# A streaming encoder step on one core: the normalization of v's last pair moved behind the first weight operands

## The chip, the cores and the metric

The kernel runs on one core of one Trainium2 chip. The metric is device time in microseconds (us) for one execution; lower is better. Five engines take part: TensorE (PE in the profile; its weight loads are PEld), VectorE (DVE), ScalarE (ACT), GpSimd (POOL) and SyncE (SP, which here only issues DMAs). Each engine runs its own instructions strictly in the order in which they were built, and waits for the others on semaphores.

## The reference, cut to what matters

One layer over 4096 prompt rows (and 32 sample rows), width 1024, everything in float32:

```python
h = rmsnorm(x, norm_g)
u, v, z_a, xb, z_b = jnp.split(h @ w_in, 5, axis=-1)        # five projections of width 1024
v_n = layernorm(v, ln_v_g, ln_v_b)
a = u * chunk_mlp(v_n, w_spatial, b_spatial) * silu(z_a)    # 128x128 mixing per head and chunk
b = pool_mix(x_ext, pos0, w_pool, pool_scale) * silu(z_b)   # trailing means, a linear map per group
y = x + concat([a, b]) @ w_out
return rmsnorm(y, final_g)
```

For this change the middle line counts: every row of v has its mean subtracted and is divided by its standard deviation, and the result is needed by the gate branch `a` only.

## The kernel before, in words

**Arithmetic.** A float32 product is made of three passes of a faster number format: each operand is split into a high part (rounded by ACT, L109 `nc.scalar.copy`) and a low part (the remainder, taken by DVE, L82 `lo_part`). Products of 2x2 blocks are formed by a scheme with seven products instead of eight. So each set of 128 output columns has seven products, numbered q = 0 to 6; one product is 12 matmuls of 128x512 (`product`, L184). Its weights are the tiles `wop`, one for each q, and some of them are sums of raw weight blocks which DVE forms first (L105, tiles `sum` and `raw`).

**Stages.** First v is computed for all rows, two row tiles (a "pair") at a time, into the SBUF tiles `vt`. Then `norms` normalizes a pair: on DVE four `BN_STATS` (L298), two `BN_AGGR` (L299), a short chain for the reciprocal root (L87 to L92), and the factors `nb` (L308); on ACT two `ACTIVATE`s of 128x1024 (L310), one for each `vt`. `Pair.store` then sends the two `vt` to DRAM (`v_all`, L489) from POOL's queue. The last two pairs are `pa` and `pb`. After v, four token blocks of 1024 rows each run through 16 "sets" of weights: 8 gate sets and 8 pool sets.

**The seam.** The first group of sets is two pool sets, called A and B here, which need no v. Their fourteen steps are interleaved by `lagged`; the first five are A0, A1, B0, A2 and B1. `prepare(n)` emits the weight operands up to step n, `LEAD = 5` is how far ahead of the products it runs, and `norms(..., behind=True)` with `store` finishes v. `tc.issue_after` and `tc.keep_in_program_order` are directions to the scheduler that orders each engine's instructions. A scheduler, not the source alone, decides the final order. As built, TensorE goes through the products in the order A0, A1, B0, B1, A3, A2, B2, A4, A5, B3, (transposes of the spatial weights WT, L823), A6, B4, B5, (L837), B6, and then the first gate set. The names of their weights are:

- before: A0 `wop_3686`, A1 `wop_3689`, B0 `wop_3721`, B1 `wop_3760`, A3 `wop_3792`, A2 `wop_3757`, B2 `wop_3814`, B5 `wop_3924`, B6 `wop_3944`
- after: the same, but B1 is `wop_3731` and A2 is `wop_3728`

**Accumulators.** Six PSUM banks hold the sums (`Combine`). q = 0 opens a bank; ACT copies it out (L158, `t<-acc`); then q = 2 and q = 4 add to the same bank. So product A2 cannot start before ACT has copied A0's sum (`t_3808<-acc_3795`). Likewise q = 6 adds to the bank that q = 3 opened, after DVE has read it (L156). For B6 that read is `t_4080<-acc_3970`.

**Queues behind the seam.** The sets' raw weights and v rows come by SP's queue: L811 loads WT, L812 the bias, L793 a few columns, L870 rows of `v_all` (after the stores of v have landed), and L877 raw weights. The loads of `raw_3962` and `raw_3964`, the weights of the second gate set, stand behind the first L870 on that queue.

Of the kernel before, what the change touches and what calls it, by code (L numbers as in the profile page):

```python
# [15 lines left out]
P = 128  # L16
# [19 lines left out]
def stream_step(ctx: ExitStack, tc, x_prompt, x_sample, state_pool, norm_g, w_in, ln_v_g, ln_v_b,  # L36
# [9 lines left out]
    nc = tc.nc  # L46
# [31 lines left out]
    def small(tag, n, rows=P):  # L78
        return smallp.tile([P, 8], F32, tag=tag, name=tag)[:rows, :n]
# [4 lines left out]
    def rsqrt(a, n, rows=P):  # L84

        y, t = small("rs_y", n, rows), small("rs_t", n, rows)
        nc.vector.tensor_single_scalar(t.bitcast(I32), a.bitcast(I32), 1, ALU.logical_shift_right)  # L87
        nc.vector.tensor_scalar(y.bitcast(I32), t.bitcast(I32), -1.0, float(0x5F3759DF), ALU.mult, ALU.add)
        for _ in range(3):
            nc.vector.tensor_tensor(t, y, y, ALU.mult)  # L90
            nc.vector.scalar_tensor_tensor(t, t, -0.5, a, ALU.mult, ALU.mult)
            nc.vector.scalar_tensor_tensor(y, t, 1.5, y, ALU.add, ALU.mult)  # L92
        return y
# [5 lines left out]
    behind, newest = [], {}  # L99
# [103 lines left out]
    def pool(name, bufs, stack=ctx, **kw):  # L203
        return stack.enter_context(tc.tile_pool(name=name, bufs=bufs, reuse_waits="tile", **kw))
# [4 lines left out]
    with ExitStack() as ph:  # L209
# [73 lines left out]
        def norms(xs_, vs_, behind=False):  # L283

            nx, nv, n = len(xs_), len(vs_), len(xs_) + len(vs_)
            rows = (xs_ + vs_)[0][1]
            a = small("na", n, rows)
            if xs_:
                ss = small("ss", nx, rows)
                for i, (xt, _) in enumerate(xs_):  # L290
                    junk = h_p.tile([P, D], BF16, tag="junk", name="junk", bufs=1)
                    nc.scalar.activation(junk[:rows], xt[:rows], AF.Square, accum_out=ss[:, i:i + 1])
            if vs_:
                st = smallp.tile([P, 2, 2, 6], F32, tag="bn", name="bn")
                mv = smallp.tile([P, 2, 2], F32, tag="mv", name="mv")
                for i, (v, _) in enumerate(vs_):
                    for z in range(2):
                        nc.vector.bn_stats(st[:rows, i, z, :], v[:rows, z * 512:(z + 1) * 512])  # L298
                    nc.vector.bn_aggr(mv[:rows, i, :], st[:rows, i].rearrange("p z c -> p (z c)"))  # L299
                nc.vector.tensor_scalar_add(a[:, nx:], mv[:rows, :nv, 1], EPS)  # L300
            if xs_:
                nc.vector.tensor_scalar(a[:, :nx], ss, 1.0 / D, EPS, ALU.mult, ALU.add)
            r = rsqrt(a, n, rows)
            for i, (xt, _) in enumerate(xs_):
                nc.vector.scalar_tensor_tensor(xt[:rows], xt[:rows], r[:, i:i + 1], g_bc[:rows], ALU.mult, ALU.mult)
            if vs_:
                nb = small("nb", nv, rows)
                nc.vector.scalar_tensor_tensor(nb, mv[:rows, :nv, 0], -1.0, r[:, nx:], ALU.mult, ALU.mult)  # L308
                for i, (v, _) in enumerate(vs_):
                    act = nc.scalar.activation(v[:rows], v[:rows], AF.Identity, scale=r[:, nx + i:nx + i + 1],  # L310
                                               bias=nb[:, i:i + 1])
                    if behind:
                        tc.keep_in_program_order(act)
# [224 lines left out]
        pa, pb = pairs[-2:]  # L538
# [261 lines left out]
    with ExitStack() as ph:  # L800
# [333 lines left out]
        def prepare(upto):  # L1134

            nonlocal done
            while done < min(upto, len(steps)):
                while loads and loads[0][0] <= done + (AHEAD if done < first[id(groups[n_sets][0])] + 7 else 6):
                    loads.pop(0)[2].load()
                s, q = steps[done]  # L1140
                s.prep[q]()
                if done in beside:
                    w, q = beside[done]
                    w.prep[q]()
                done += 1

        tokens[0].ops = first_ops
        for s in groups[0]:
            loads.pop(0)[2].load(nc.gpsimd)
        for n, pair in ((2, pa), (3, pb)):  # L1150
            prepare(n)
            norms([], [(v, P) for v in pair.v], behind=True)
            pair.store(nc.gpsimd)
        with tc.issue_after(newest["lo"]):
            prepare(LEAD)
        v_stack.close()
        t_p = pool("t_p", 10, ph)
        cn_p = pool("cn_p", 1, ph)
# [156 lines left out]
```

## Time and profile before

| what | value |
|---|---|
| time, median of 3 runs | 2327.71 us (2327.01 to 2328.79) |
| profiled execution | 2331.34 us |
| its span on the core | 2329.6 us |
| PE busy | 2312.3 us, 99% |
| DVE busy | 1761.1 us, 76% |
| ACT busy | 893.6 us, 38% |
| granted TensorE clock, mean | 0.999 |

How to read the profile's lines: a timeline row has the start in us from the span's start, the length in us, the engine, the line of the kernel, the operation, the tiles (out<-in), shapes, and xN for a run of equal instructions; in square brackets stands the idle time of the engine before it and who ended that. SPq is a DMA issue on SP's queue. A row of the waits has the total in us, the number of times, and the longest. The row "PEclk" of a page and the column PEclk of a table by stretches are the granted clock of TensorE as a share of full speed.

### The profile page before, as it was taken

How to read it: one execution, taken by the hardware profiler on the slowest of the kernel's cores; microseconds unless marked ns; L12 is line 12 of the kernel's file. 1: busy time of each engine (PE TensorE's matmuls, PEld its weight loads, DVE VectorE, ACT ScalarE, POOL GpSimd, SP SyncE). 2: the span in 40 equal slices, each digit the busy share in tenths (PEclk: the TensorE clock that was granted, in tenths of full speed). 3: DMA queues.
4: the chain of work that ended last, by engine and by line, in shares of the span. 5: the costliest groups of instructions: out<-in, count | busy, mean ns of one | idle time of the engine just before them, and what ended most of it. 6: DMA issues, size and time to landing. Idle time of an engine off the chain costs nothing.

```text
span 2329.6 us, 30101 instructions
## 1 busy us (share of the span) xinstructions
PE 2312.3 (99%) x10722; PEld 1891.8 (81%) x10722; DVE 1761.1 (76%) x3171; ACT 893.6 (38%) x1560; POOL 229.4 (10%) x357
## 2 busy tenths in 40 slices
PE   8999999999999999999999999999999999999998
PEld 6888888878778888788878888888888777887887
DVE  6887777868787866787767967768876666588887
ACT  6554544334334333443434433434322222233343
POOL 1000000000131002221000211001100000000000
PEclk9999999999999999999999999999999999999999
DMA  9877877445548454566544393535485665856552
GB/s 309 303 271 276 294 244 248 136 161 172 170 153 334 149 179 140 197 225 230 190 159 143 118 331 107 194 118 167 180 340 169 214 205 197 334 163 204 178 168 90
DMA packets 320365, 474.95 MB, mean 204 GB/s; under 512 B 27324, under 2 KB 226492, under 8 KB 318424
## 3 DMA queue, kind: packets, MB, share of 16 engines
q1 hardware_dynamic: 269016, 383.96, 48.3%
q0 software_dynamic: 21936, 74.14, 8.7%
q10 hardware_dynamic: 29264, 14.94, 2.4%
q8 instruction: 84, 1.38, 0.2%
q14 instruction: 65, 0.53, 0.1%
HBM read 303.51 MB, written 169.47 MB: 203 GB/s over the span
## 4 chain that ended last, share of the span: by engine, by line
PE 97%; DMA 1%; DVE 1%; ACT 0%; issue 0%; SPq 0%; ACTq 0%; DVEq 0%
PE acc L184 65%; PE acc L665 9%; PE acc L667 9%; PE acc L666 9%; PE sp L918 2%; PE tr L428 1%; PE acc L192 1%; DMA vt<-in_w_in_dram 1%; PE acc L259 1%; PE more L192 1%; DMA op<-in_w_in_dram 0%; DMA wops<-wop 0%; DVE wop L82 0%; PE tr L380 0%; DVE slot L82 0%
## 5 line engine op out<-in xcount | busy, mean ns | idle before, releaser
L184 PE MATMUL acc<-slot,wop 128*128 128x512 f32 x5376 | 1240.7, 391 | 0.8 <-DVE wop L82 0.4
L184 PEld LDWEIGHTS acc<-slot,wop 128*128 128x128 f32 x5376 | 1003.4, 188 | 225.7 <-DVE t L156 9.6
L82 DVE TENSOR_TENSOR wop<-raw,wop 128x512 fp32r<-128x512 f32 x520 | 353.9, 685 | 47.2 <-ACT wop L109 39.2
L109 ACT CAST wop<-raw 128x512 fp32r<-128x512 f32 x360 | 221.1, 622 | 332.2 <-PE acc L184 253.0
L665 PE MATMUL acc<-slot,wop 128*128 128x512 f32 x892 | 348.4, 391 | 0.0
L667 PE MATMUL acc<-slot,wop 128*128 128x512 f32 x892 | 347.1, 389 | 0.0
L666 PE MATMUL acc<-slot,wop 128*128 128x512 f32 x892 | 347.0, 389 | 0.0
L184 PE MATMUL acc<-slot,op 128*128 128x512 f32 x1344 | 323.2, 395 | 1.3 <-ACT op L434 1.1
L184 PEld LDWEIGHTS acc<-slot,op 128*128 128x128 f32 x1344 | 247.8, 188 | 52.7 <-ACT op L434 1.6
L156 DVE TENSOR_TENSOR t<-acc,t 128x512 f32<-128x512 f32 x256 | 175.5, 685 | 139.6 <-ACT t L165 102.5
L677 DVE TENSOR_TENSOR y<-acc,y 128x512 f32<-128x512 f32 x243 | 164.4, 687 | 134.6 <-PE acc L667 133.6
L665 PEld LDWEIGHTS acc<-slot,wop 128*128 128x128 f32 x892 | 167.4, 188 | 44.7 <-ACT wop L628 10.1
L628 ACT CAST wop<-raw 128x512 fp32r<-128x512 f32 x160 | 99.4, 621 | 253.6 <-PE acc L667 231.5
L667 PEld LDWEIGHTS acc<-slot,wop 128*128 128x128 f32 x892 | 167.4, 188 | 34.9
L666 PEld LDWEIGHTS acc<-slot,wop 128*128 128x128 f32 x892 | 167.4, 188 | 34.5
L82 DVE TENSOR_TENSOR wop<-sum,wop 128x512 fp32r<-128x512 f32 x208 | 142.3, 686 | 66.0 <-ACT wop L109 64.9
L926 POOL DMA_DIRECT2D abT<-t x128 | 69.3, 542 | 798.5 <-DVE t L936 542.3
L109 ACT CAST wop<-sum 128x512 fp32r<-128x512 f32 x144 | 89.1, 622 | 148.9 <-PE acc L184 99.1
L947 DVE TENSOR_TENSOR t<-t 128x527 f32<-128x527 f32 (+3 forms) x160 | 111.1, 695 | 0.4
L165 ACT COPY t<-acc 128x512 f32<-128x512 f32 x64 | 37.5, 586 | 126.9 <-PE acc L184 126.9
L628 ACT CAST wop<-sum 128x512 fp32r<-128x512 f32 x64 | 39.8, 621 | 105.3 <-PE acc L667 70.6
L920 DVE SCALAR_TENSOR_TENSOR t<-sp,lvg,bias 128x512 f32<-128x512 f32 x64 | 47.7, 745 | 42.0 <-PE sp L918 41.9
(201 smaller groups left out, 1875.7 us busy)
## 6 DMA issues: line engine op xcount, KB each, us to landing
raw<-in_w_in_dram SPq DMA_DIRECT2D x134, 512.0 KB, 4.7
xops<-op SPq DMA_DIRECT2D x100, 512.0 KB, 6.5
slot<-xops SPq DMA_DIRECT2D x44, 1024.0 KB, 9.5
abT<-t POOLq DMA_DIRECT2D x128, 256.0 KB, 3.0
raw<-abT SPq DMA_DIRECT2D x64, 512.0 KB, 5.2
wops<-wop SPq DMA_DIRECT2D x56, 512.0 KB, 3.4
slot<-wops SPq DMA_DIRECT2D x14, 2048.0 KB, 9.6
raw<-comb SPq DMA_DIRECT2D x38, 512.0 KB, 4.4
```

The source lines that it names most:

```text
L82: return nc.vector.tensor_tensor(out, src, hi.bitcast(F32), ALU.subtract)
L109: pair = nc.scalar.copy(hi, src), lo_part(lo, src, hi)
L156: add = lambda o, x, y: nc.vector.tensor_tensor(o, x, y, ALU.add)
L184: mm(acc, stationary(s, k), moving(m, k), start=fresh and n == 0, stop=n == len(terms) - 1, skip_group_check=True)
L628: nc.scalar.copy(t[:, 0], src)
L665: mm(acc, x[:, 0, k, :], w[:, k, 0, c], start=fresh and k == 0, stop=False, skip_group_check=True)
L666: mm(acc, x[:, 0, k, :], w[:, k, 1, c], start=False, stop=False, skip_group_check=True)
L667: mm(acc, x[:, 1, k, :], w[:, k, 0, c], start=False, stop=k == 3, skip_group_check=True)
L677: nc.vector.tensor_tensor(y, self.acc[bank], y, ALU.add)
L920: nc.vector.scalar_tensor_tensor(t1[:, :HALF].rearrange("p (a c) -> p a c", c=P), sp, lg, bias[:, h:h + 1, :].broadcast_to([P, 4, P]), ALU ...
L926: nc.gpsimd.dma_start(abT[row, :, t0:t0 + HALF], t[:, :HALF])
L947: tt(nxt[:, lo:HALO + m], s[:, lo:HALO + m], s[:, lo - step:HALO + m - step], ALU.add)
```

## The change

The loop over the two pairs is written out, and for `pb` the order is turned: before, `norms` and `store` of `pb` came right after `prepare(3)` and ahead of `prepare(LEAD)`; now `prepare(LEAD)` comes first, `norms` of `pb` follows inside the same `issue_after` block, and the store follows that. Nothing is computed differently and no instruction is added or removed.

```diff
-        for n, pair in ((2, pa), (3, pb)):
-            prepare(n)
-            norms([], [(v, P) for v in pair.v], behind=True)
-            pair.store(nc.gpsimd)
+        prepare(2)
+        norms([], [(v, P) for v in pa.v], behind=True)
+        pa.store(nc.gpsimd)
+        prepare(3)
         with tc.issue_after(newest["lo"]):
             prepare(LEAD)
+            norms([], [(v, P) for v in pb.v], behind=True)
+        pb.store(nc.gpsimd)
```

What stands on DVE where `pb`'s chain ended, before. `vt_3355` and `vt_3356` are `pb`'s two tiles; `rs_t`, `rs_y` and `nb_3747` are its chain, `raw` and `sum` the raw blocks and block sums of sets A and B:

```order
L91 SCALAR_TENSOR_TENSOR rs_t_3735<-rs_t_3735,na_3724 128x2
L82 TENSOR_TENSOR wop_3721<-raw_3682,wop_3721 128x512
L92 SCALAR_TENSOR_TENSOR rs_y_3734<-rs_t_3735,rs_y_3734 128x2
L105 TENSOR_TENSOR sum_3753<-raw_3680,raw_3678 128x512
L90 TENSOR_TENSOR rs_t_3735<-rs_y_3734 128x2
L105 TENSOR_TENSOR sum_3754<-raw_3680,sum_3753 128x512
L91 SCALAR_TENSOR_TENSOR rs_t_3735<-rs_t_3735,na_3724 128x2
L105 TENSOR_TENSOR raw_3680<-raw_3680 128x512
L92 SCALAR_TENSOR_TENSOR rs_y_3734<-rs_t_3735,rs_y_3734 128x2
L105 TENSOR_TENSOR sum_3810<-raw_3684,raw_3682 128x512
L308 SCALAR_TENSOR_TENSOR nb_3747<-mv_3726,rs_y_3734 128x2
L82 TENSOR_TENSOR wop_3757<-sum_3754,wop_3757 128x512
```

Four large operations (128x512) stand between B0's low part `wop_3721` and `nb_3747`; by then the four `BN_STATS` are done. The low part of A2 comes behind `nb`.

What stands there now, from B0's low part on:

```order
L82 TENSOR_TENSOR wop_3721<-raw_3682,wop_3721 128x512
L105 TENSOR_TENSOR sum_3724<-raw_3680,raw_3678 128x512
L298 BN_STATS bn_3735<-vt_3355 128x6
L105 TENSOR_TENSOR sum_3725<-raw_3680,sum_3724 128x512
L298 BN_STATS bn_3735<-vt_3355 128x6
L298 BN_STATS bn_3735<-vt_3356 128x6
L82 TENSOR_TENSOR wop_3728<-sum_3725,wop_3728 128x512
L82 TENSOR_TENSOR wop_3731<-raw_3682,wop_3731 128x512
L299 BN_AGGR mv_3736<-bn_3735 128x2
L298 BN_STATS bn_3735<-vt_3356 128x6
L105 TENSOR_TENSOR raw_3680<-raw_3680 128x512
L299 BN_AGGR mv_3736<-bn_3735 128x2
```

All four `BN_STATS` now stand behind B0's low part, and the low parts of A2 and B1 ahead of the chain. The chain's steps follow, each between two large operations (`sum_3810`, `wop_3792`, `raw_3684`, `raw_3678`, `sum_3811`, `raw_3682`), and it ends in eight small steps in a row with `nb_3757` as the last, ahead of `t_3808<-acc_3817`.

ACT's order around `pb`'s two `ACTIVATE`s (before it is the same, with the names of before):

```order
L109 CAST wop_3792<-raw_3680 128x512
L310 ACTIVATE vt_3355<-vt_3355,nb_3757,rs_y_3744 128x1024
L310 ACTIVATE vt_3356<-vt_3356,nb_3757,rs_y_3744 128x1024
L158 COPY t_3808<-acc_3795 128x512
L109 CAST wop_3814<-sum_3811 128x512
```

The `ACTIVATE`s have kept their place on ACT: the copy of A0's sum still stands behind them, and B2's cast behind that.

Further on, DVE's order where the second gate set's first sum `sum_4240` stood before, behind L955:

```order
L105 TENSOR_TENSOR raw_3834<-raw_3834 128x512
L156 TENSOR_TENSOR t_3941<-acc_3894,t_3939 128x512
L82 TENSOR_TENSOR wop_4022<-raw_3832,wop_4022 128x512
L947 TENSOR_TENSOR t_4043<-t_3808 128x527
L105 TENSOR_TENSOR raw_3832<-raw_3832,sum_4053 128x512
L156 TENSOR_TENSOR t_3939<-acc_3947,t_3939 128x512
L947 TENSOR_TENSOR t_4045<-t_4043 128x525
L82 TENSOR_TENSOR wop_4056<-sum_4053,wop_4056 128x512
L955 SCALAR_TENSOR_TENSOR t_4045<-t_4045,t_3808 128x496
L105 TENSOR_TENSOR sum_4240<-raw_3964,raw_3962 128x512
L824 MEMSET WT_3787 64x4x64
```

And now:

```order
L82 TENSOR_TENSOR wop_3967<-raw_3832,wop_3967 128x512
L105 TENSOR_TENSOR sum_4240<-raw_3964,raw_3962 128x512
L156 TENSOR_TENSOR t_3941<-acc_3894,t_3939 128x512
L82 TENSOR_TENSOR wop_4022<-raw_3832,wop_4022 128x512
L947 TENSOR_TENSOR t_4043<-t_3808 128x527
L105 TENSOR_TENSOR raw_3832<-raw_3832,sum_4053 128x512
L156 TENSOR_TENSOR t_3939<-acc_3947,t_3939 128x512
L947 TENSOR_TENSOR t_4045<-t_4043 128x525
L82 TENSOR_TENSOR wop_4056<-sum_4053,wop_4056 128x512
L955 SCALAR_TENSOR_TENSOR t_4045<-t_4045,t_3808 128x496
L105 TENSOR_TENSOR sum_4241<-raw_3964,sum_4240 128x512
L824 MEMSET WT_3787 64x4x64
```

`sum_4240`, which waits for the loads of `raw_3964` and `raw_3962`, has moved up by eight large operations, ahead of `t_3941<-acc_3894`, and `sum_4241` has taken its old place. The order of TensorE, POOL and SP is unchanged; on ACT a few casts further on changed places with copies.

## The prediction

> **What bounds the kernel now.** I read the page first, then the waits of TensorE, then the timelines of PE, ACT, DVE and the queues around the seam between v and the first sets. The page, with its span, its PE row and the chain that ended last:
>
> ```profile
> span 2329.6 us, 30101 instructions
> PE 2312.3 (99%) x10722; PEld 1891.8 (81%) x10722; DVE 1761.1 (76%) x3171; ACT 893.6 (38%) x1560; POOL 229.4 (10%) x357
> ...
> PE 97%; DMA 1%; DVE 1%; ACT 0%; issue 0%; SPq 0%; ACTq 0%; DVEq 0%
> ```
>
> TensorE is busy 99% of the span and makes 97% of the chain. So a microsecond counts only if TensorE itself starts later or earlier, and one lost at the seam has nowhere to be made up, since what follows is bound by TensorE too. The waits of TensorE, longest first:
>
> ```profile
> PE tr L380 <- DMA vt<-in_w_in_dram: 3.0, 1, 3.0
> ...
> PE acc L184 <- DVE wop L82: 0.4, 1, 0.4
> ```
>
> Nearly all of its waiting belongs to the start of the program. At the seam it waits once, 0.4 us, for a low part that DVE makes. That is the most the change can win. TensorE's timeline there:
>
> ```profile
> 385.83 4.47 PE L184 MATMUL acc<-slot,op 128*128 128x512 f32 x19
> 390.14 8.78 PE L184 MATMUL acc<-slot,wop 128*128 128x512 f32 x38
> 399.36 18.89 PE L184 MATMUL acc<-slot,wop 128*128 128x512 f32 x82 [0.44 <-DVE wop L82]
> ```
>
> The last product of v runs into A0 at 390.14 without a pause. 38 matmuls are A0, A1, B0 and two matmuls of B1; then it stands 0.44 us until B1's low part is there. Matmuls follow each other every 0.228 us, so A2, 22 matmuls after 399.36, began at 404.4.
>
> A measurement of this kernel can tell about 0.2%, 4.7 us, from no change.
>
> **Part 1: the wait that goes.** DVE after v's last sum, up to the low parts of A2 and B1:
>
> ```profile
> 390.34 0.69 DVE L156 TENSOR_TENSOR vt<-acc,vt 128x512 f32<-128x512 f32 x1 [0.29 <-PE acc L184]
> 390.95 1.28 DVE L82 TENSOR_TENSOR wop<-raw,wop 128x512 fp32r<-128x512 f32 x2
> ...
> 393.12 0.17 DVE L300 TENSOR_SCALAR na<-mv 128x2 f32<-128x2 f32 x1
> 393.32 0.17 DVE L87 TENSOR_SCALAR rs_t<-na 128x2 int32<-128x2 int32 x1
> ...
> 395.20 0.15 DVE L92 SCALAR_TENSOR_TENSOR rs_y<-rs_t,rs_y 128x2 f32<-128x2 f32 x1
> 395.27 0.68 DVE L105 TENSOR_TENSOR sum<-raw 128x512 f32<-128x512 f32 x1
> 395.87 0.15 DVE L90 TENSOR_TENSOR rs_t<-rs_y 128x2 f32<-128x2 f32 x1
> ...
> 397.94 0.15 DVE L308 SCALAR_TENSOR_TENSOR nb<-mv,rs_y 128x2 f32<-128x2 f32 x1
> 398.01 0.68 DVE L82 TENSOR_TENSOR wop<-sum,wop 128x512 fp32r<-128x512 f32 x1
> ```
>
> Three prices come from here. A large operation takes its place for 0.60 to 0.61 us (390.34 to 390.95, 395.27 to 395.87), a small one ahead of a large one for 0.07 (395.20 to 395.27; where the next must wait for its input, 0.12), and a small one that feeds the next small one for 0.20 (393.12 to 393.32). In the new order B1's low part is the eighth large operation from B0's on instead of standing behind the chain. ACT's timeline says when that series can start:
>
> ```profile
> 391.90 0.60 ACT L109 CAST wop<-raw 128x512 fp32r<-128x512 f32 x1
> 396.76 0.63 ACT L109 CAST wop<-sum 128x512 fp32r<-128x512 f32 x1 [4.26 <-PE acc L184]
> ...
> 398.33 2.37 ACT L310 ACTIVATE vt<-vt,nb,rs_y 128x1024 f32<-128x1024 f32 x2
> 400.61 0.56 ACT L158 COPY t<-acc 128x512 f32<-128x512 f32 x1
> ```
>
> The cast of B0's high part ends at 392.50, so B0's low part starts at 392.54 and B1's ends at 392.54 + 8 x 0.605 = 397.4, well ahead of the 398.5 at which TensorE wants it. The wait of 0.44 us goes, and A2 could start at 390.14 + 60 x 0.228 = 403.8.
>
> **Part 2: what is late next.** `nb` of the last pair. From B0's low part to `nb_3757` DVE now has 16 large operations (in before's order four were left at that point), 7 small ones between large ones, and eight small ones in a row at the end: 392.54 + 16 x 0.605 + 7 x 0.09 + 7 x 0.20 + 0.15 = 404.4, against 398.1 before. DVE, which never idles in this stretch, only turned the order round: six microseconds of preparation have moved in front of `nb`. ACT's order has not followed. Its two ACTIVATEs wait for `nb` and start at 404.45 instead of 398.33; the copy of A0's sum behind them starts 2.28 later (398.33 to 400.61) at 406.73 and ends at 407.3. A2 adds to that bank, so it starts at about 407.4 instead of 404.4. In before's trace the copy ended at 401.2, 3.2 us early; this slack was the cover, and it is used up. Net of part 1, the first term is **+3.0 us**. Its ends: if the seven small operations cost nothing and a large one 0.60, `nb` is 0.7 earlier, +2.3; if each costs 0.20, it is 0.8 later, +3.8. Everything queued behind the ACTIVATEs on ACT, B2's cast first, is late too, but the casts follow at 0.6 us each and a product lasts 2.73, so they are ahead again at once.
>
> **Part 3: the store and what is queued behind it.** POOL issues the store, SP waits for it to land before it reads v back, and the loads of the next raw weights stand behind that:
>
> ```profile
> 400.99 0.89 POOL L489 DMA_DIRECT2D v_all<-vt  x1 [0.25 <-ACT vt L310]
> ...
> 406.84 0.32 SPq L870 DMA_DIRECT2D raw<-v_all  x1
> 407.27 2.97 SPq L877 DMA_DIRECT2D raw<-in_w_in_dram  x2
> ```
>
> How long such loads take to land, from the DMA issues of 385 to 440 us (median, the last column) and from the operations on the tile `raw`:
>
> ```profile
> raw<-in_w_in_dram SPq DMA_DIRECT2D x4, 512.0 KB, 4.9
> ...
> DMA to landing us min/median/max: 3.5/5.0/5.8
> ```
>
> The second store is now issued at 407.1, and if it lands as before (5.85 us later) L870 goes at 412.95 and the two loads at 413.4 and 413.8. Even if it lands sooner, `raw_3964` cannot be loaded before about 413, when DVE has read the old content of its buffer for B5 (the ninth operation from 407.4 on at 0.61 us: 412.9). It lands 4.9 us later; I take 418.5, between 417.3 (413.8 + 3.5) and 419.6 (+ 5.8). Before, DVE reached the sum that reads it only after both loads had landed; now that sum stands eight large operations earlier and DVE will stop at it. What DVE owes TensorE behind it is the read that frees B6's bank. The rows of before for that piece, and B6 on TensorE:
>
> ```profile
> 418.28 0.68 DVE L105 TENSOR_TENSOR sum<-raw 128x512 f32<-128x512 f32 x1
> 419.06 0.27 DVE L824 MEMSET WT<- 64x256 f32 x1
> ...
> 426.22 0.68 DVE L156 TENSOR_TENSOR t<-acc,t 128x512 f32<-128x512 f32 x1
> ...
> 428.46 3.78 PE L184 MATMUL acc<-slot,wop 128*128 128x512 f32 x14
> ```
>
> From L824 to the end of that read DVE needs 7.84 us (419.06 to 426.90) without a pause, and it ended 1.6 us before B6. In the new order ten large operations stand between the landing and L824: 9 x 0.605 + 0.78 = 6.2. So the read ends at 418.5 + 6.2 + 7.8 = 432.5, while B6, pushed by part 2, wants to start at 428.46 + 3.0 = 431.5. Second term: **+1.0 us**, from 0 (landing at 417.3) to 2.1 (419.6).
>
> The sum is +4.0 us. Against the profiled execution's 2331.34 us (span 2329.6 and 1.7 around it) that is 2335.3; the median of the runs lies 3.6 below the profiled one, and carried over to it the forecast is 2327.7 + 4.0 = 2331.7, or +0.17%. By the ends of the terms alone it goes from +2.3 to +5.9.
>
> **TensorE's clock.** Part 2 makes a pause of 403.9 to 407.4, 3.5 us, the longest of the program. The trace has one such pause, at the start:
>
> ```profile
> 11.40 1.27 PE L380 MATMUL tr<-ident,vt 128*128 128x128 f32 x8 [3.02 <-DMA vt<-in_w_in_dram]
> ```
>
> The clock around it and in a later stretch, from the table by stretches (PE's busy time comes first, the granted clock is the third number from the end):
>
> ```profile
> 8.70:12.12 3.42, 0.72 (x7) 0.75 (x8) 0.06 (x1) 0.31 (x1) 0.00 (x0) 1.00 1.10 360
> 12.12:15.53 3.41, 3.41 (x12) 2.75 (x10) 1.28 (x2) 0.00 (x0) 0.00 (x0) 0.50 0.81 242
> ...
> 46.25:49.66 3.41, 1.99 (x12) 1.57 (x13) 3.41 (x4) 3.38 (x8) 1.10 (x3) 1.00 0.22 77
> ```
>
> After the stretch in which PE was busy 0.72 of 3.42 us, the clock was halved for 3.41 us; after one with 1.99 of 3.41 it was not. So the new pause may or may not halve it, by how it falls on such stretches; if it does, up to 3.41 us run at half speed and 1.7 are lost. The Trainium skill's page "TensorE: Matmul & The Clock Gate", Part 1, has this as a rule: the gate judges free-running windows of about 3.4 us and halves the clock after an idle one, and its closing table tells authors to leave no idle gap over some 3 us. By that rule the change is a worse bargain than by my sum. The trace agrees as far as it shows the window's length and one halving; how much work in a window prevents it lies between 21% and 58% busy here. This is the second rival.
>
> **The rivals.**
>
> *The late load decides (slower).* The place is DVE's stop at `sum_4240`, the price one for one in the landing of `raw_3964`. With landing at 419.6, the second term is 2.1 and the sum +5.1: 2332.8. It turns the result to slower by over 0.2% from a landing of about 419.2 on. For it: the loads are now issued back to back with L870, all of 512 KB. Against it: the slot loads that still ran beside the old store are over by then.
>
> *The clock halves.* After the pause 1.2 to 1.7 us are lost to the low clock. B6 then wants to start only at 433, when DVE's read is done, so the second term goes: 3.0 + 1.7 = +4.7 at most, 2332.4, right on the edge of 0.2%.
>
> *No pause at A2.* If `nb` were ready by 401.2, only the gain of part 1 were left: -0.4, 2327.3. Against it stand 16 large operations of 0.6 us; nothing speaks for it but that the order of issue could be looser than it reads.
>
> **How the numbers follow.** Forecast (both terms, clock unchanged): 0.50. Late load: 0.17. Clock halved: 0.26, half of it on either side of the edge. No pause: 0.05. The last 0.02 is for what I do not see, a gain included. Slower by over 0.2%: 0.17 + 0.13 and 0.07 from the forecast's own upper end, 0.37. Faster: 0.02. The same: 0.61. The range for 8 in 10: from the first term's low end with nothing of the second, +2.3, to the late load's +5.1, each widened by some 0.8 us for the spread of the runs shown (2327.01 to 2328.79), which gives 2329.3 to 2333.6.
>
> **What would show it.** Right: `nb`'s L308 at about 404.4 and the ACTIVATEs right behind it; a wait of PE's L184 for ACT's copy L158 of 3 to 4 us near 407; no wait near 399; DVE idle ahead of `sum<-raw` for some 3 us near 418, ended by a DMA; a second wait of PE for DVE's L156 near 432; from there on a constant shift. Wrong: no PE wait near 407 (then ACT or DVE did not keep the order), no DVE pause near 418 (the loads were early), or a granted clock of 0.50 right behind the pause, which is the rival. A shift that goes on growing behind 440 would mean a queue that I left out.

## The result and the profile after

| kernel | median us | runs | ratio to before, 95% interval |
|---|---|---|---|
| before | 2328.02 | 18 | |
| after | 2332.34 | 18 | 1.0019, 1.0012 to 1.0026 |
| after, on a second chip (before 2328.61 there) | 2333.49 | 11 | 1.0020, 1.0011 to 1.0029 |

The change costs 4.3 us, and 4.9 on the second chip; forecast were 4.0. The change is slower than before, since both intervals lie above 1; whether by more than 0.2% stays open, since both intervals reach over it. Among the runs below, one execution of h_sum_late (4740.25 us) and one of before beside it (2563.02) stand far above all others and count in no ratio. The profiled execution of after took 2332.16 us, with a span of 2330.4. The engines' row of its page:

```profile
PE 2312.6 (99%) x10722; PEld 1891.7 (81%) x10722; DVE 1760.8 (76%) x3171; ACT 893.2 (38%) x1560; POOL 223.9 (10%) x357
```

The bound and the busy times are those of before. TensorE's waits, the longest first:

```profile
PE acc L184 <- ACT t L158: 3.3, 1, 3.3
...
PE tr L380 <- DMA vt<-in_w_in_dram: 0.8, 1, 0.8
```

The wait for ACT's copy is new and is the longest of the program; the wait for DVE's L82 is gone. The second row is a warning: the very first load cost before's profiled execution 3.0 us and this one 0.8, which has nothing to do with the change. So A0 started at 390.14 in before's profile and at 386.59 in this one, and spans of single executions can't be compared. From here on positions at the seam are counted from the start of A0. TensorE's timeline of after:

```profile
386.59 13.76 PE L184 MATMUL acc<-slot,wop 128*128 128x512 f32 x60
403.67 15.54 PE L184 MATMUL acc<-slot,wop 128*128 128x512 f32 x60 [3.32 <-ACT t L158]
...
430.12 11.18 PE L184 MATMUL acc<-slot,wop 128*128 128x512 f32 x48
```

Sixty matmuls run through, then TensorE stands 3.32 us and A2 starts 17.08 after A0 (before: 9.22 + 22 x 0.228 = 14.24). The row of 430.12 is B6, 43.53 after A0 (before: 428.46, 38.32). What stood ahead of the two, from the same timeline, all engines:

```profile
400.58 0.16 DVE L308 SCALAR_TENSOR_TENSOR nb<-mv,rs_y 128x2 f32<-128x2 f32 x1
400.78 2.37 ACT L310 ACTIVATE vt<-vt,nb,rs_y 128x1024 f32<-128x1024 f32 x2 [5.00 <-DVE nb L308]
...
403.05 0.56 ACT L158 COPY t<-acc 128x512 f32<-128x512 f32 x1
403.44 0.89 POOL L489 DMA_DIRECT2D v_all<-vt  x1 [0.25 <-ACT vt L310]
...
408.85 1.02 SPq L877 DMA_DIRECT2D raw<-in_w_in_dram  x2
...
416.01 0.69 DVE L105 TENSOR_TENSOR sum<-raw 128x512 f32<-128x512 f32 x1 [3.10 <-DMA raw<-in_w_in_dram]
```

`nb` is ready 14.0 after A0 (before 7.8). ACT had stood idle for it for 5 us, then scales, then copies A0's sum, and the next matmul starts with the copy's end. Below, the second chain: the store, the two loads behind it, DVE's stop at `sum_4240`. DVE restarts 29.42 after A0, and 14.11 us later B6 starts: that is the work that it owes ahead of B6's bank. TensorE's clock around the pause, by stretches (columns as in the prediction):

```profile
401.55:404.97 3.42, 1.30 (x6) 1.08 (x7) 1.32 (x3) 3.42 (x6) 1.88 (x3) 1.00 0.47 139
404.97:408.38 3.41, 3.41 (x10) 2.65 (x9) 3.41 (x6) 3.03 (x7) 0.00 (x0) 0.50 0.93 257
```

The stretch with 1.30 us of work was followed by one at half clock, in which 3.41 us do the work of 1.7. So the clock's rival happened as well. Three things thus push B6 in this execution: the pause (2.8), the clock (1.7) and a rest (0.7). Which of them carry the time?

### The profile page after: what moved, and what is told of

Same layout as the page of the kernel before. It is cut to its first block, busy times and chain, and to the rows that moved or that the text cites. A ratio compares the mean times of both kernels' runs of the same rounds, so it can differ in the third digit from the quotient of the medians.

```text
span 2330.4 us, 30102 instructions
## 1 busy us (share of the span) xinstructions
PE 2312.6 (99%) x10722; PEld 1891.7 (81%) x10722; DVE 1760.8 (76%) x3171; ACT 893.2 (38%) x1560; POOL 223.9 (10%) x357
## 4 chain that ended last, share of the span: by engine, by line
PE 81%; DVE 1%; ACT 0%; DMA 0%; issue 0%; ACTq 0%; DVEq 0%
PE acc L184 51%; PE acc L665 9%; PE acc L667 9%; PE acc L666 9%; PE sp L918 2%; PE acc L192 1%; PE more L192 1%; DVE wop L82 0%; DMA raw<-in_w_in_dram 0%; ACT vt L310 0%; DVE sum L105 0%; DVE t L156 0%; DVE raw L105 0%; DVE WT L826 0%; DVE bn L298 0%
## 5 line engine op out<-in xcount | busy, mean ns | idle before, releaser
L82 DVE TENSOR_TENSOR wop<-raw,wop 128x512 fp32r<-128x512 f32 x520 | 355.2, 687 | 49.3 <-ACT wop L109 42.4
L156 DVE TENSOR_TENSOR t<-acc,t 128x512 f32<-128x512 f32 x256 | 176.0, 688 | 143.3 <-ACT t L165 102.6
L82 DVE TENSOR_TENSOR wop<-sum,wop 128x512 fp32r<-128x512 f32 x208 | 142.7, 688 | 60.0 <-ACT wop L109 59.1
```

Source lines behind the costliest of these rows:

```text
L82: return nc.vector.tensor_tensor(out, src, hi.bitcast(F32), ALU.subtract)
L156: add = lambda o, x, y: nc.vector.tensor_tensor(o, x, y, ALU.add)
```

## The experiments

The theory, formed from these rows: two chains run side by side, and B6 starts at the later of two moments. One is TensorE's own series (A0 plus 38.3, plus what the pause and the clock take). The other is DVE's restart after the late load, plus 14.1 us of DVE's work. The rivals: the waits add up; the clock is a loss of its own; or the clock doesn't matter. All runs were timed beside before on the same chip, except g_half_fill, which is one execution. Where an edit changes line numbers, it is said.

### p_pool_scale: the copy freed, nb still late

GpSimd does the two scalings of `pb`; no other engine's order changes (the scaling is L311 here).

```diff
-                    act = nc.scalar.activation(v[:rows], v[:rows], AF.Identity, scale=r[:, nx + i:nx + i + 1],
-                                               bias=nb[:, i:i + 1])
+                    rb = r[:, nx + i:nx + i + 1], nb[:, i:i + 1]
+                    act = (eng.tensor_scalar(v[:rows], v[:rows], *rb, ALU.mult, ALU.add) if eng else nc.scalar.activation(v[:rows], v[:rows], AF.Identity, scale=rb[0], bias=rb[1]))
...
-            norms([], [(v, P) for v in pb.v], behind=True)
+            norms([], [(v, P) for v in pb.v], behind=True, eng=nc.gpsimd)
```

(Left out: `eng=None` in the head of `norms`.)

> The changed kernel, but pb's two scalings (the two ACTIVATEs of L310) are done by GpSimd instead of ACT; every other engine keeps its order, nb stays where the change put it. ACT's copy of A0's sum then has nothing late ahead of it. Theory (the two waits overlap: B6 cannot start before the late raw weights land plus 14.1 us of DVE's work, whatever A2 does): PE's wait for ACT of 3.3 us at A2 goes, but the wait for DVE at B6 takes its place with 3 to 5 us, and the time stays within 1 us of the changed kernel's, 4 to 5 us above before (more if GpSimd is slower than ACT's 1.2 us for one scaling, one for one). Rival (the two terms add up, as the prediction had it): 3.0 us are gained, only 1.0 is left, about 2329. Rival (the late copy is not what A2 waits for): a wait of 3 us stays at A2.

Measured: 2334.67 us against 2328.18, ratio 1.0030 (1.0018 to 1.0041). Its timeline:

```profile
388.19 27.37 PE L184 MATMUL acc<-slot,wop 128*128 128x512 f32 x120
...
402.46 3.34 POOL L311 TENSOR_SCALAR vt<-vt,rs_y,nb 128x1024 f32<-128x1024 f32 x2 [11.23 <-DVE nb L308]
...
419.15 0.69 DVE L105 TENSOR_TENSOR sum<-raw 128x512 f32<-128x512 f32 x1 [7.40 <-DMA raw<-in_w_in_dram]
...
420.50 10.04 PE L184 MATMUL acc<-slot,wop 128*128 128x512 f32 x36 [4.07 <-DVE t L156]
...
433.27 3.01 PE L184 MATMUL acc<-slot,wop 128*128 128x512 f32 x12 [1.00 <-DVE t L156]
```

120 matmuls run without a stop: A2's wait is gone, so the late copy was its whole cause. Yet nothing is gained. DVE, no longer held up at the copy of A0's sum (2.91 us in after), comes to the load earlier and stands 7.40 us there, and TensorE waits for it 4.07 us at A6 and 1.00 at B6. GpSimd takes 1.67 us for a scaling where ACT takes 1.18, and as it issues the stores itself, both go out behind its second scaling; that puts the loads later: DVE restarts 30.96 after A0 instead of 29.42, and B6 starts 45.08 after A0, again 14.12 behind the restart. That the waits add up is refuted: with the first one gone, the second grew and took its place. The expected bound of 1 us from the changed kernel was missed for GpSimd's slower work, which the expectation had left open.

### h_sum_late: DVE's stop removed, the pause left

```diff
-                s.prep[q]()
+                if s is groups[2][0] and q == 2:
+                    with tc.issue_after(newest["wt"]):
+                        s.prep[q]()
+                else:
+                    s.prep[q]()
```

`newest["wt"]` is the MEMSET of WT (L824); the line that notes it is left out here.

> The changed kernel, but the sum of raw weights at which DVE stopped (sum_4240) is held back behind the work on WT (L824), where before had it; A2's wait for ACT is left as it is. Theory: DVE no longer stops near 413 to 416, PE's wait for DVE at B6 goes, and what is left is the pause at A2: 2.7 us over before where TensorE's clock stays full behind the pause, up to 4.4 where it is halved for 3.4 us. Rival (terms add up): 1.0 us less than the changed kernel, 3.0 over before. Rival (the late load decides alone): back to before's time within 0.5 us.

Measured: 2333.00 against 2328.18 (2332.76 without the execution far above), ratio 1.0020 (1.0011 to 1.0029). Its timeline of TensorE, then the stretches behind the pause:

```profile
388.85 13.76 PE L184 MATMUL acc<-slot,wop 128*128 128x512 f32 x60
405.93 16.57 PE L184 MATMUL acc<-slot,wop 128*128 128x512 f32 x60 [3.32 <-ACT t L158]
...
432.73 3.56 PE L184 MATMUL acc<-slot,wop 128*128 128x512 f32 x13
```

```profile
404.81:408.23 3.42, 2.30 (x5) 1.82 (x6) 2.32 (x4) 3.42 (x7) 1.65 (x3) 0.50 0.58 164
408.23:411.64 3.41, 3.41 (x9) 2.63 (x8) 3.41 (x7) 1.95 (x5) 0.84 (x20) 0.50 0.96 286
```

There is no wait ahead of B6 any more, and still B6 starts 43.88 after A0, and the time is close to that of the changed kernel. In this profile the pause fell so that two stretches were halved, 6.83 us, where the expectation had reckoned with one: the clock took what DVE's stop had left. It is a profile of an execution of 2334.96 us, the slowest of the ten. The load itself is as late as in after (issued 22.24 after A0, there 22.26); only the sum that reads it stands so far back again that the load has landed by then.

### g_fill and g_sum_fill: the clock held up

Fourteen matmuls fill the pause, in the changed kernel (g_fill) and with the sum held back too (g_sum_fill). The bank `spin` is read by nobody, so this is extra work. A second piece of the edit, left out here, writes A2 behind B1 and A3, where TensorE had it anyway.

```diff
+                if n == 0 and m == 5:
+                    spin = sp_tile().rearrange("p a c -> p (a c)")
+                    for k in range(14):
+                        tc.keep_in_program_order(mm(spin, s.ops[3][:, 0, 0, :], s.tok.moving(3, 0, 0),
+                                                    start=True, stop=True))
                 s.product(cs[id(s)], q)
```

> The changed kernel with 14 extra matmuls of 128x512 on TensorE between A3 and A2 (14 x 0.228 = 3.2 us), into a PSUM bank that nobody reads; the order of all else is the same. They fill the pause in which A2 waits for ACT, so TensorE's clock should stay full; A2 starts at the same 17.1 us after A0. Theory (the waits overlap: B6 starts no earlier than 14.2 us after raw_3964 has landed, 43.5 us after A0): PE's wait for DVE at B6 grows from 0.7 to about 2.4 us and the time does not change, 4 to 5 us above before. Rival (the halved clock is a loss of its own): the wait at B6 stays at 0.7 and the kernel is 1.7 us faster than the changed one. Rival (filling keeps nothing): the clock is halved all the same.

Measured: 2333.32 against 2328.61, ratio 1.0019 (1.0010 to 1.0028). The timeline of g_fill, with the filling matmuls as L1196:

```profile
387.03 13.76 PE L184 MATMUL acc<-slot,wop 128*128 128x512 f32 x60
400.63 3.33 PE L1196 MATMUL sp<-slot,wop 128*128 128x512 f32 x14
404.12 13.92 PE L184 MATMUL acc<-slot,wop 128*128 128x512 f32 x60 [0.16 <-ACT t L158]
...
415.95 0.69 DVE L105 TENSOR_TENSOR sum<-raw 128x512 f32<-128x512 f32 x1 [3.35 <-DMA raw<-in_w_in_dram]
...
430.06 6.19 PE L184 MATMUL acc<-slot,wop 128*128 128x512 f32 x26 [1.24 <-DVE t L156]
```

Sixty matmuls take 13.92 us behind the filled pause where they took 15.54 in after: the clock is full. But what is gained there is given back as a wait for DVE at B6, 14.11 behind the restart once more (43.03 after A0). The row's 1.24 counts from the modelled end of the matmuls of L837 ahead of it; by B6's start it is 1.8 (against g_sum_fill, next). That is less than the expected 2.4, since the load came 0.5 us sooner than in after's profile.

> The same 14 matmuls, and the sum of raw weights held back behind L824 as in h_sum_late. Now nothing is late at B6, so what the clock takes shows in the time. Theory (pause 2.7, halved clock 1.7 for each 3.41 us of it, in most executions one or two): full clock behind A2, B6 at about 40.6 us after A0 (43.9 in h_sum_late's profile), time 2.7 us above before, 1.7 to 2.5 below the median of h_sum_late. Rival (the clock is halved too seldom to count): the same median as h_sum_late, 4 to 5 above before.

Measured: 2331.63 against 2328.61, ratio 1.0011 (1.0002 to 1.0020). Its timeline (the filling matmuls between the first two rows):

```profile
387.51 13.76 PE L184 MATMUL acc<-slot,wop 128*128 128x512 f32 x60
...
404.60 13.92 PE L184 MATMUL acc<-slot,wop 128*128 128x512 f32 x60 [0.16 <-ACT t L158]
...
428.74 7.63 PE L184 MATMUL acc<-slot,wop 128*128 128x512 f32 x31
```

With DVE's stop and the halved clock both out of the way only the pause is left: B6 at 41.23 after A0 (expected 40.6), 2.9 above before's 38.32, and 3.0 us in the time (expected 2.7). Against h_sum_late (4.6 above before without its far execution) the full clock is worth 1.6. The intervals of the two overlap, so by the times alone this is not shown; the position of B6 in the profiles (43.88 and 41.23) shows where it comes from.

### p_both: neither the copy nor DVE's stop

The edits of p_pool_scale and h_sum_late together; `nb` is as late as in the changed kernel.

> Both at once: pb's scalings on GpSimd and the sum held back behind L824. nb is as late as in the changed kernel. Theory (nothing else is late): no wait over 0.5 us near A2 or B6, no halved clock there, and the time is before's or up to 0.4 us less (the wait for B1's low part stays gone). Rival (a further queue is late, or GpSimd's work slows DVE): over 1 us is left, with a new wait of PE between A0 and the first gate set.

Measured: 2327.47 against 2328.18, ratio 0.9997 (0.9988 to 1.0006). TensorE, and the two loads:

```profile
387.71 27.37 PE L184 MATMUL acc<-slot,wop 128*128 128x512 f32 x120
...
411.90 1.01 SPq L877 DMA_DIRECT2D raw<-in_w_in_dram  x2
...
425.46 10.87 PE L184 MATMUL acc<-slot,wop 128*128 128x512 f32 x46
```

No pause, no stop, B6 at 37.75, 0.57 earlier than before's: the wait for B1's low part stays gone. The two waits, for the late copy and for the late load, with what the clock adds to the first, are the whole loss. Neither `nb` nor the load has to come earlier for that: the loads are issued 24.19 after A0 here, later than the 22.26 of after. So the second wait needed two things, a late load and the sum that the scheduler had moved up on DVE by eight large operations; back in its old place, the sum finds the load landed.

### s_inside_first and n_outside: what in the diff does it

The diff turns two things at once: the order of writing, and whether `pb`'s normalization lies in the `issue_after` block. One kernel keeps the block and turns the order back, the other keeps the order and leaves the block.

```diff
         with tc.issue_after(newest["lo"]):
+            norms([], [(v, P) for v in pb.v], behind=True)
             prepare(LEAD)
-            norms([], [(v, P) for v in pb.v], behind=True)
```

> The change turned round inside its block: pb's normalization is written ahead of prepare(LEAD) again, as before had it, but inside the issue_after block; the store stays behind. In the built order nb then stands one place earlier on DVE than in the changed kernel, and six behind before's. Theory (the block delays nb, and not the place behind the preparation): nb at 13.5 us after A0, a wait of 2.5 to 3 us for ACT at A2, short waits of together 0.3 to 0.9 us at B1 and A3, the same stop of DVE at the load; 3.5 to 5 us above before. Rival (the order of writing decides): before's time within 0.5 us.

Measured: 2332.27 against 2328.61, ratio 1.0015 (1.0006 to 1.0024). From the timeline:

```profile
387.15 9.38 PE L184 MATMUL acc<-slot,wop 128*128 128x512 f32 x40
...
400.67 0.16 DVE L308 SCALAR_TENSOR_TENSOR nb<-mv,rs_y 128x2 f32<-128x2 f32 x1
...
403.75 13.90 PE L184 MATMUL acc<-slot,wop 128*128 128x512 f32 x60 [2.17 <-ACT t L158]
...
415.54 0.69 DVE L105 TENSOR_TENSOR sum<-raw 128x512 f32<-128x512 f32 x1 [3.30 <-DMA raw<-in_w_in_dram]
...
429.65 6.65 PE L184 MATMUL acc<-slot,wop 128*128 128x512 f32 x28 [1.22 <-DVE t L156]
```

Written first, `nb` is still 13.52 after A0. A2's wait is 2.17, less than the 2.5 to 3 expected. The clock stayed full behind this shorter pause; B6 starts at 42.50, 14.11 behind the restart.

```diff
         with tc.issue_after(newest["lo"]):
             prepare(LEAD)
-            norms([], [(v, P) for v in pb.v], behind=True)
+        norms([], [(v, P) for v in pb.v], behind=True)
```

> The normalization of pb is written behind prepare(LEAD), as in the changed kernel, but outside the issue_after block. In the built order nb then stands three large DVE operations (1.8 us) later than in before instead of 6.2 us. Theory (only how late nb is counts, with 3.2 us of slack at the copy of A0's sum): no pause at A2, no stop of DVE at the load, and the wait of 0.44 us for B1's low part goes: 0 to 0.4 us below before. Rival (being behind the preparation costs as such, by ACT's queue or the store): 1 us or more above before.

Measured: 2328.86 against 2328.18, ratio 1.0004 (0.9995 to 1.0013). From the timeline:

```profile
386.63 8.78 PE L184 MATMUL acc<-slot,wop 128*128 128x512 f32 x38
395.70 18.89 PE L184 MATMUL acc<-slot,wop 128*128 128x512 f32 x82 [0.29 <-DVE wop L82]
...
396.24 0.15 DVE L308 SCALAR_TENSOR_TENSOR nb<-mv,rs_y 128x2 f32<-128x2 f32 x1
...
398.71 0.56 ACT L158 COPY t<-acc 128x512 f32<-128x512 f32 x1
```

Outside the block `nb` comes 9.61 after A0, 1.8 later than before, the copy ends 12.64 after A0, still ahead of A2's 14.1, and the time is before's. So the block is what puts `nb` late, whichever is written first. The wait for B1's low part shrank only from 0.44 to 0.29, so of the expected gain hardly any was there to see.

### d7_more_ahead: the dose doubled

```diff
         with tc.issue_after(newest["lo"]):
-            prepare(LEAD)
+            prepare(7)
             norms([], [(v, P) for v in pb.v], behind=True)
```

> The dose doubled: seven weight operands are prepared ahead of pb's normalization in the block, instead of five. In the built order three more large DVE operations stand ahead of nb, 1.9 us. Theory (each microsecond that nb is late beyond the 3.2 us of slack delays A2, and through the store the landing of raw_3964 and B6, one for one): nb at 15.9 us after A0, PE's wait for ACT at A2 5.2 us, B6 at 45 to 46 us after A0 (43.0 to 44.1 in the changed kernel), time 6 to 7 us above before. Rival (the waits of the changed kernel come from the block or the store's place, not from the number of operations): the same 4 to 5 us.

Measured: 2336.59 against 2327.81, ratio 1.0037 (1.0024 to 1.0050). From the timeline:

```profile
386.65 13.76 PE L184 MATMUL acc<-slot,wop 128*128 128x512 f32 x60
405.61 15.69 PE L184 MATMUL acc<-slot,wop 128*128 128x512 f32 x60 [5.20 <-ACT t L158]
...
417.66 0.69 DVE L105 TENSOR_TENSOR sum<-raw 128x512 f32<-128x512 f32 x1 [2.66 <-DMA raw<-in_w_in_dram]
...
433.14 3.25 PE L184 MATMUL acc<-slot,wop 128*128 128x512 f32 x13 [1.06 <-DVE t L156]
```

A2's wait is 5.20 as expected. B6 comes 46.49 after A0, later than the expected 45 to 46, and the time is 8.8 above before instead of 6 to 7: here 15.48 us of DVE's work stand between the restart and B6, since two more large operations have moved in between (2 x 0.61). The first chain answers one for one to the 1.88 us that `nb` is later than in after; the second gives 1.59 at the restart and 1.37 of work behind it.

### after_again and g_half_fill: when the clock is halved

> The changed kernel once more. Theory: A2's wait 3.3 us, B6 at the landing of raw_3964 plus 14.2 us whether or not the clock is halved behind the pause; 4 to 5 us above before. Rival (the halved clock adds itself): 1.7 us between executions with and without it.

The time stands in the first table. TensorE and DVE's restart:

```profile
387.34 13.76 PE L184 MATMUL acc<-slot,wop 128*128 128x512 f32 x60
404.43 16.76 PE L184 MATMUL acc<-slot,wop 128*128 128x512 f32 x60 [3.32 <-ACT t L158]
...
416.49 0.69 DVE L105 TENSOR_TENSOR sum<-raw 128x512 f32<-128x512 f32 x1 [1.60 <-DMA raw<-in_w_in_dram]
...
431.40 4.92 PE L184 MATMUL acc<-slot,wop 128*128 128x512 f32 x19
```

Sixty matmuls take 16.76 us: two stretches are halved. B6 comes 44.06 after A0, 14.91 behind the restart and without a wait: here the clock decides, and the theory's "whether or not" is wrong for this case. The late load puts B6 at 43.3 at the earliest; one halved stretch doesn't reach that far, two do, by 0.8 us.

The last kernel is g_sum_fill with `range(7)`, so that half the pause is filled.

> As g_sum_fill, with 7 extra matmuls instead of 14: the pause at A2 is half filled and 1.7 us long. By the profiles so far a pause of 3.32 us halved the clock behind it each time, for one or for two stretches of 3.41 us, and pauses of 2.17 and 1.24 us did not. Expected: full clock, B6 at about 41.2 us after A0 as in g_sum_fill. Rival (any pause of over a microsecond may halve it, by where it falls): 3.41 us at 0.5 behind A2 and B6 at 42.9.

One execution: 2331.79 us. The pause, and the stretch that holds it:

```profile
403.34 13.93 PE L184 MATMUL acc<-slot,wop 128*128 128x512 f32 x60 [1.74 <-ACT t L158]
```

```profile
401.82:405.24 3.42, 1.90 (x8) 1.59 (x9) 1.92 (x4) 3.42 (x7) 1.89 (x3) 1.00 0.63 180
```

A pause of 1.74 us left the clock full, and B6 started at 41.23 after A0 as in g_sum_fill.

## Why the prediction held, point by point

The positions of B6 show the rule; all are counted from A0, and the last column but one is the restart plus 14.11 (15.48 for d7_more_ahead). The 14.11 was read off after and the 15.48 off d7_more_ahead itself, so these two rows test nothing; the others with a value there do. The clock's column counts us at half clock, some of them inside the pause:

| kernel | wait at A2 | clock halved | load allows B6 | B6 started |
|---|---|---|---|---|
| before | 0 | 0 | | 38.32 |
| p_both | 0 | 0 | | 37.75 |
| g_sum_fill | (filled) | 0 | | 41.23 |
| s_inside_first | 2.17 | 0 | 42.50 | 42.50 |
| g_fill | (filled) | 0 | 43.03 | 43.03 |
| after | 3.32 | 3.41 | 43.53 | 43.53 |
| after_again | 3.32 | 6.83 | 43.26 | 44.06 |
| h_sum_late | 3.32 | 6.83 | | 43.88 |
| p_pool_scale | 0 | 3.41 (at A6) | 45.07 | 45.08 |
| d7_more_ahead | 5.20 | 6.83 | 46.49 | 46.49 |

One caution on the last column. A B6 that did not wait is recorded about 0.3 us early: to the next L918 row behind it there are 11.33 us in before and 11.32 in g_sum_fill, but 11.01 in after and in g_fill. So after's shift against before, 5.2 at B6, is 4.9 at that row, nearer to the 4.3 and 4.9 of the times. At the end of the span it is still 4.4 (2330.4 - 386.59 against 2329.6 - 390.14), so nothing further on goes on growing.

- **The bound and part 1 held.** TensorE is busy 99%, the wait for B1's low part went in after and p_both, and its worth of 0.4 us is below what the timing can tell.
- **Part 2 held in mechanism and size.** `nb` came 13.99 after A0 (forecast 404.4, that is 14.26), A2 at 17.08 (forecast 17.26): the first term is 2.8, not 3.0. p_pool_scale shows that the copy behind the ACTIVATEs is the whole of this wait.
- **Part 3 had the right mechanism and a term that was too small.** Without a halved clock the late load costs 43.03 - 41.23 = 1.8 (g_fill against g_sum_fill; 1.5 at the L918 row, 1.7 in the medians), not 1.0. The mis-sized number is the landing. The first of the two loads was issued 22.26 after A0, a microsecond earlier than forecast (413.4, 23.26), since the store landed sooner; but DVE restarted 7.2 us after that issue, where the forecast had 5.1 from a median of four loads. Why this pair took longer is not shown. In after the restart is 29.42 after A0, which is the upper end of the forecast's own bounds (419.6, that is 29.46), and so the place of its late-load rival. The rest of this step, 14.0 us of DVE's work behind the landing, was measured as 14.11.
- **The form of the sum held.** The second term was counted from where the first leaves B6, so the two were never two independent losses; my expectations read that sum as if each could be taken out for its own price, and p_pool_scale and h_sum_late refuted that reading.
- **The clock was given too small a chance (0.26).** It was halved in both profiles of the changed kernel and in the three others with a wait of over 3 us. That the time still fit is the late load's doing: the prediction's remark that the second term goes when the clock is halved is, but for a rest of 0.7, what after's profile shows, and even two halved stretches bring B6 only 0.8 us later in after_again (1.1 at the L918 row). For executions without a profile only the mean granted clock is on record, to three digits, and halved stretches at the program's start count in it as well. In after_again the six at 0.997 took 2333.43 to 2335.47 us and the three at 0.999 took 2332.08 to 2332.91, medians 1.1 apart; in before beside it, 0.998 and 0.999 have the same median within 0.01. In after itself two of 18 stand at 0.997 and one at 1.000, which took 2331.24 and has no room for a halved stretch (0.0005 of the span is 1.2 us; a stretch loses 1.7). So the clock's part varies from one execution to the next. The Trainium skill's page "TensorE: Matmul & The Clock Gate", Part 1, has the gate judge free-running windows of about 3.4 us; the trace agrees (ahead of the program's end every halved stretch lasted 3.41 us or twice that, and by where the pause fell it was one or two), but the window needn't be idle: 1.30 us of work in it did not prevent it.
- **The number.** 2331.7 against 2332.34: the first term 0.2 too high, the second 0.5 to 0.8 too low, the clock left out; 0.3 of the difference is before's own median, which went from 2327.71 (3 runs) to 2328.02 (18). It is right as a time, and it is the late-load and clock rivals together that after's profile looks like, more than the case called likeliest. The second wait of TensorE, for DVE's L156, that was named as a sign is missing from after's list of waits; it stands in g_fill (1.24), where the clock is full. That the number came so close although the clock was left out is luck in part: the late load covered most of what the clock took.

Left open: whether the loads were held by the queue behind the store or by their buffer, which came free at nearly the same moment, was not tried apart. Why the scheduler moved the sum up is not shown either. Neither p_both nor n_outside can be told from before.

## What to carry to other kernels

When work is moved behind other work on one engine, look at every engine that waits for it in order: here DVE did the same work as before, but ACT stood with a cheap copy behind a late scaling, and a load stood behind a late store while the sum that needs it had moved up. Where two late chains end at the same instruction, only the later one is paid, so taking one of them out buys little, and the next must be priced before it is tried. And read what the scheduler built, not the order of the source lines: the block decided here, not the line.

## What the runs showed of the hardware

In these traces TensorE's clock is granted in stretches of 3.41 us, and whether the next is halved follows from the work in the one before, with a sharp edge. The cases nearest to the edge, from p_pool_scale and from the start of h_sum_late:

```profile
414.85:418.26 3.41, 1.59 (x12) 1.17 (x10) 0.00 (x0) 0.00 (x0) 0.00 (x0) 1.00 1.13 355
418.26:421.67 3.41, 1.17 (x5) 0.99 (x6) 2.52 (x5) 1.15 (x2) 0.00 (x0) 1.00 0.42 151
421.67:425.08 3.41, 3.41 (x10) 2.63 (x9) 3.41 (x6) 1.14 (x2) 0.00 (x0) 0.50 0.00 0
```

```profile
43.00:46.41 3.41, 1.41 (x9) 0.96 (x8) 3.20 (x9) 3.34 (x9) 1.09 (x3) 1.00 0.55 213
46.41:49.83 3.42, 3.42 (x13) 2.81 (x12) 3.42 (x6) 3.42 (x8) 0.56 (x1) 0.50 0.25 85
```

The wait in the stretch from 43.00, from the timeline of h_sum_late:

```profile
46.02 0.79 PE L428 MATMUL tr<-ident,xt 128*128 128x128 f32 x4 [2.00 <-DVE xt L305]
```

A stretch at full clock with 1.59 us of busy PE kept it, one with 1.41 lost it. At half clock 2.30 us of busy PE (h_sum_late) kept it halved, 3.41 brought it back; counted as work at full clock those are 1.15 and 1.7. So the edge lies between 1.41 and 1.59 us of 3.41, a little under half. So it is the work in a stretch that counts, and not the length of a pause: the stretch from 43.00 lost the clock with a wait of 2.0 us in it, while waits of 2.17 (s_inside_first) and 1.74 us (g_half_fill), which were spread over stretches otherwise, did not. A pause of 3.32 us cost one stretch (after) or two (after_again, h_sum_late), by how it fell; by the edge found here, an estimate, it costs none when two stretches share it about evenly.
